# Gate and up projection of two prompt groups as one two by two block product with seven block products

## The chip, the cores and the metric

The kernel runs on one NeuronCore of a Trainium2 chip. The metric is the device time of one execution in microseconds. The engines are TensorE (PE in the profile, with its weight loads as PEld), VectorE (DVE), ScalarE (ACT), GpSimd (POOL) and SyncE (SP), which here only issues DMA transfers. The engines run side by side, each takes its own instructions in a fixed order, and semaphores join them.

## What is computed

One encoder layer is applied to 1536 tokens of width 1024: a prompt of 1024 and a sample of 512 tokens, with the same weights and a modulation vector of their own each. The change lies in the second half of the layer, and what surrounds it is this:

```python
x = x + gt1 * rms_norm(mix, g_post_mix)          # mix: output projection, 1024 x 1024
h = rms_norm(x, g_pre_ffn) * (1.0 + sc2) + sh2
gate, up = jnp.split(jnp.dot(h, w_gu), 2, axis=-1)   # w_gu: 1024 x (2 * 2816)
f = jnp.dot(jax.nn.silu(gate) * up, w_down)          # w_down: 2816 x 1024
return x + gt2 * rms_norm(f, g_post_ffn)
```

## The kernel before

The tokens are three groups of 512 (`TG`): groups 0 and 1 are the prompt, group 2 the sample. Activations lie transposed, channels on the 128 partitions and the 512 tokens of a group along the row, so that one matmul takes a 128 x 128 weight block and 512 columns. All weights and activations are float32. To keep their precision, `split` (lines 137 to 139) writes each operand as two fp32r tiles: ACT casts the high part, and DVE (or POOL, where the caller says so) subtracts it from the source for the low part. `mm3` (line 158) then makes three matmuls for each 128-row chunk of K: high weight with high activation, high with low, low with high. A block over K = 1024 is 8 chunks, 24 matmuls, and fills one PSUM bank; PSUM has 4 banks under the tag mm, 2 under st and 2 under pv.

`weights` (line 141) loads a weight tile through SP into `wraw` (4 buffers of 128 x 512) and splits it into `whl` (4 buffers), so PE runs one block of 1024 behind the splits.

`out_proj(gi)` makes the output projection of a group, 8 blocks (`mt`). `post` (line 794) evacuates each block twice on ACT (lines 806 and 807: scaled into `sc`, squared into `ta`) and adds up the squares on DVE (line 190). Work that belongs to a group but need not hold PE up is a generator on `self.back`, of which `tick(n)` issues n steps after each block. After an output projection such a generator, `behind`, follows: row scale (`rms`: a small matmul, a reciprocal root on DVE L215 and POOL L216, and `spread` over ACT L227, a matmul and ACT L232 into a tile `rs`, 2 buffers), then for each of 8 chunks a multiplication by the row scale (L819), the addition of the residual from DRAM (L820), the store of `x1` (L821), a square on ACT (L823) and the sum of squares on DVE (L838); at its end `rs2[gi]`, the row scale of the second norm, from a second `rms`.

`ffn_in(gi)` (line 890, through `modulate`, line 374) loads the chunks of `x1` into `xc` (3 buffers), scales them (DVE L380, ACT L382) and splits them (ACT, POOL) into 8 tiles of `h` (16 buffers of 128 x 2 x 512). For group 0 it is woven step by step with the `behind` of group 1, during the output projection of group 2; for groups 1 and 2 it runs during the down projection of the group before.

`ffn(gi)` (line 894) has two stages. Gate and up: for each of 22 columns j a gate and an up block over `h2`, then silu (ACT L907, DVE L908) and the product with up (DVE L909), split at once into a tile that stays in SBUF (`HID` names the buffers it borrows). Down: 8 blocks of 22 chunks, 66 matmuls each, into `post`. The last quarter of the adaLN modulation (`ada_rest((5,))`) is fed in between columns 4 to 7.

What is written here is not the order on the engines. The tile framework plans the instructions: on each engine the next is, among those whose inputs and buffers are ready by its own model, the one that stands first in the program; that order is then fixed, and a buffer's next use waits for its last reader. Matmuls of a later block can so come ahead of one whose operand is late.

## Time and profile before

| | us |
|---|---|
| median of 3 runs (1886.78 to 1887.4) | 1886.98 |
| the profiled execution | 1886.02 |
| its span | 1884.2 |

| engine | busy us | share of the span |
|---|---|---|
| PE | 1846.7 | 98% |
| PEld | 1471.2 | 78% |
| DVE | 928.3 | 49% |
| ACT | 690.6 | 37% |
| POOL | 149.0 | 8% |

The span runs from the first to the last instruction of the profiled execution; times in views are microseconds from its start. The group projections and attention fill it to about 610 us, the three output projections to about 751, and then come the three groups' gate and up stages (from about 751, 1130 and 1499) and down stages. A matmul's duration in a view contains its way through the array, and neighbouring ones overlap: their cost to a full PE is the distance from start to start. The same holds for DVE instructions, which overlap a little.

### The profile page before, as it was taken

To read this page: it belongs to the slowest core of one execution; us is meant where nothing else is said; L and a number is where in the kernel's file an instruction comes from. 1 tells how busy PE (TensorE), PEld (TensorE's weight loads), DVE (VectorE), ACT (ScalarE), POOL (GpSimd) and SP (SyncE) were. 2 spreads that over 40 slices of the span, in tenths; PEclk is the share of its full clock that TensorE was granted. 3 is DMA by queue.
4 is the path that set the end of the run, shared out by engine and by line. 5 is a ranking of instruction groups with operands and counts; after the bars stand their busy time and mean duration, and the time that the engine had idled before them with its cause. 6 is when DMAs were issued, how large, how long until landed. Compare 5 with 4: busy or idle time off the path is not lost.

```text
span 1884.2 us, 23515 instructions
## 1 busy us (share of the span) xinstructions
PE 1846.7 (98%) x8866; PEld 1471.2 (78%) x8866; DVE 928.3 (49%) x1447; ACT 690.6 (37%) x1180; POOL 149.0 (8%) x102
## 2 busy tenths in 40 slices
PE   7999999999999999999999999999999999999997
PEld 7777876766777777878888888888888888888886
DVE  4334864473795467834443427444442374444223
ACT  3511642152444456533333423333342333333222
POOL 1400100010122012100000100000020000000001
PEclk9999999999999999999999999999999999999999
DMA  8112322234353367642223435322243342222432
GB/s 340 38 55 76 110 95 93 90 118 134 111 176 114 132 218 217 213 162 92 97 94 108 123 94 181 109 95 95 95 122 97 95 169 97 93 95 95 137 96 75
DMA packets 123682, 228.30 MB, mean 121 GB/s; under 512 B 13744, under 2 KB 19120, under 8 KB 123568
## 3 DMA queue, kind: packets, MB, share of 16 engines
q1 hardware_dynamic: 123424, 226.73, 36.2%
q8 instruction: 69, 1.13, 0.2%
q14 instruction: 45, 0.37, 0.1%
q10 hardware_dynamic: 144, 0.07, 0.0%
HBM read 206.30 MB, written 20.45 MB: 120 GB/s over the span
## 4 chain that ended last, share of the span: by engine, by line
PE 59%; DVE 0%; POOL 0%; DVEq 0%; ACT 0%; issue 0%
PE pmm L156 58%; PE pst L156 1%; DVE sc L861 0%; DVE sc L863 0%; POOL rq L216 0%; DVE whl L139 0%; DVEq L1054 0%; ACT tb L227 0%; DVE rq L215 0%
## 5 line engine op out<-in xcount | busy, mean ns | idle before, releaser
L156 PE MATMUL pmm<-h,whl 128*128 128x512 f32 x5772 | 1384.2, 398 | 11.7 <-ACT h L138 5.2
L156 PEld LDWEIGHTS pmm<-h,whl 128*128 128x128 f32 x5772 | 1079.1, 189 | 288.6 <-issue 22.6
L139 DVE TENSOR_TENSOR whl<-wraw,whl 128x512 fp32r<-128x512 f32 (+1 forms) x548 | 386.0, 707 | 461.3 <-ACT whl L138 458.1
L138 ACT CAST whl<-wraw 128x512 fp32r<-128x512 f32 (+1 forms) x548 | 333.2, 609 | 674.4 <-PE pmm L156 558.5
L139 POOL TENSOR_TENSOR h<-tb,h 128x512 fp32r<-128x512 f32 x40 | 59.6, 1497 | 554.9 <-ACT h L138 546.7
L156 PE MATMUL pmm<-qk,whl 128*128 128x512 f32 x414 | 100.0, 394 | 0.0
L908 DVE SCALAR_TENSOR_TENSOR ta<-ta,pmm 128x512 f32<-128x512 f32 x66 | 45.4, 687 | 110.8 <-ACT ta L907 110.7
L156 PEld LDWEIGHTS pmm<-qk,whl 128*128 128x128 f32 x414 | 77.8, 188 | 18.3
L907 ACT ACTIVATE ta<-pmm 128x512 f32<-128x512 f32 x66 | 39.5, 598 | 141.4 <-PE pmm L156 141.4
L909 DVE SCALAR_TENSOR_TENSOR ta<-ta,pmm 128x512 f32<-128x512 f32 x66 | 45.3, 687 | 79.2 <-PE pmm L156 79.0
L190 DVE TENSOR_TENSOR acc<-acc,ta 128x512 f32<-128x512 f32 x55 | 38.6, 702 | 55.4 <-ACT ta L807 44.3
L156 PE MATMUL pst<-qk 64*128 64x128 f32 (+3 forms) x384 | 61.7, 320 | 0.7 <-DVE st L782 0.7
L156 PEld LDWEIGHTS pst<-qk 64*128 64x128 f32 (+1 forms) x384 | 45.6, 187 | 20.1 <-issue 14.3
L216 POOL TENSOR_TENSOR rq<-rq,half 128x4 f32<-128x4 f32 (+1 forms) x11 | 11.7, 1068 | 526.6 <-DVE rq L215 521.9
L382 ACT ACTIVATE tb<-tb,mod,G 128x512 f32<-128x512 f32 x48 | 38.8, 815 | 39.8 <-DVE tb L380 36.0
L156 PE MATMUL pmm<-v,whl 128*128 128x512 f32 x207 | 51.4, 392 | 0.0
L139 POOL TENSOR_TENSOR h<-xc,h 128x512 fp32r<-128x512 f32 x24 | 33.7, 1414 | 171.3 <-ACT h L138 155.1
L806 ACT ACTIVATE sc<-pmm,G 128x512 f32<-128x512 f32 x47 | 32.2, 686 | 40.8 <-PE pmm L156 40.6
L156 PEld LDWEIGHTS pmm<-v,whl 128*128 128x128 f32 x207 | 38.8, 188 | 8.8
L460 DVE SCALAR_TENSOR_TENSOR sc<-cst,pst 128x512 f32<-128x512 f32 (+2 forms) x56 | 26.9, 512 | 37.8 <-PE pst L156 37.7
L620 POOL PARTITION_ALL_REDUCE st<-st x8 | 21.0, 2637 | 224.1 <-DVE st L556 224.1
L156 PE MATMUL pst<-h,qk 128*128 128x128 f32 x256 | 31.8, 286 | 7.0 <-DMA h<-in_wada 6.8
(163 smaller groups left out, 1299.6 us busy)
## 6 DMA issues: line engine op xcount, KB each, us to landing
wraw<-in_wgu SPq DMA_DIRECT2D x264, 256.0 KB, 2.7
wraw<-in_wdn SPq DMA_DIRECT2D x120, 256.0 KB, 2.6
wraw<-in_win SPq DMA_DIRECT2D x84, 256.0 KB, 2.8
xc<-in_wada SPq DMA_DIRECT2D x48, 256.0 KB, 3.7
wraw<-in_wout SPq DMA_DIRECT2D x48, 256.0 KB, 3.0
xc<-in_x SPq DMA_DIRECT2D x40, 256.0 KB, 3.6
xc<-x SPq DMA_DIRECT2D x40, 256.0 KB, 3.7
h<-in_wada SPq DMA_DIRECT2D x16, 512.0 KB, 9.6
```

Source lines behind the costliest of these rows:

```text
L138: self.nc.scalar.copy(hi, src)
L139: (eng or self.nc.vector).tensor_tensor(out=lo, in0=src, in1=hi.bitcast(F32), op=ALU.subtract)
L156: self.nc.tensor.matmul(out, lhsT, rhs, start=start, stop=stop, skip_group_check=True)
L190: nc.vector.tensor_tensor(out=acc, in0=acc, in1=t, op=ALU.add)
L216: nc.gpsimd.tensor_tensor(out=y, in0=y, in1=self.half8[:, :n], op=ALU.pow)
L382: nc.scalar.activation(t, t, AF.Identity, bias=sh[:, kc, c:c + 1], scale=G[:, kc, c:c + 1])
L460: self.nc.vector.scalar_tensor_tensor(out=out, in0=table, scalar=slope, in1=ps, op0=ALU.mult, op1=ALU.add)
L620: self.nc.gpsimd.partition_all_reduce(x[:, :grp.n], x[:, :grp.n], channels=128, reduce_op=RED.max)
L806: nc.scalar.activation(ys[-1][:, mt % 2], ps, AF.Copy, scale=G[:, mt, c:c + 1])
L907: nc.scalar.activation(t, ps[0], AF.Tanh, scale=0.5)
L908: nc.vector.scalar_tensor_tensor(out=t, in0=t, scalar=1.0, in1=ps[0], op0=ALU.add, op1=ALU.mult)
L909: nc.vector.scalar_tensor_tensor(out=t, in0=t, scalar=0.5, in1=ps[1], op0=ALU.mult, op1=ALU.mult)
```

## The change

Gate and up of column j are a weight block of 2 x 2 (A11, A12: the two K halves of gate; A21, A22: those of up) against an activation block of 2 x 2 (B11, B12: the first K half of groups 0 and 1; B21, B22: the second). Instead of eight products of half blocks seven are made, of sums and differences of the A and of the B (the form named after Strassen and Winograd), and the four results come out of sums of the seven. Groups 0 and 1 go through gate and up together; group 2 goes as before.

- `wino_in` takes the place of the two `ffn_in`: for each of 4 pairs of chunks it makes the tiles of B11, T2, B21, T3, T1 (20 tiles, in the buffers that `OPS` names) and stores T4 and B22 in DRAM (`late`). It stands on `self.back` behind the `behind` of group 1, no longer woven with it, and runs during the third output projection. `wino_late` loads T4 and B22 again and splits them into `h` once the third output projection is through.
- `wino_weights` forms the four sums of the weights on DVE and splits seven operands, in `whl` and `sc` by turns. Raw tiles come in two sets by the parity of j: `wraw` with one of `xc`, and `sd`.
- `wino_products` makes the seven products, 12 matmuls each, into three PSUM banks, some of them added to what a bank holds.
- `ffn_up` reads the banks between the products, makes the silu and the gating step of both groups, and stores the activations in DRAM (`hid`). The split of the activations is no longer there.
- `ffn_down(gi)` loads the 22 activations of a group, splits them into the buffers of `HIDP` and makes the down projection, which is the old one under the name `down`.

```diff
@@ __init__
+        self.hid = self.dr.tile([2, NJ, 128, TG], F32, name="hid")
+        self.late = self.dr.tile([2, 4, 128, TG], F32, name="late")
...
+    OPS = ["h"] * 8 + ["qk"] * 6 + ["v"] * 3 + ["vm"] * 2 + ["sc"]
+    HIDP = ["h"] * 8 + ["qk"] * 6 + ["v"] * 3 + ["vm"] * 2 + ["sc"] + ["st"] * 2
...
+    def wino_in(self, ops):
+
+        nc = self.nc
+        rs = [self.spread(self.rs2[gi], True) for gi in range(2)]
+        for o in ("B11", "T2", "B21", "T3", "T1", "T4", "B22"):
+            ops[o] = []
+        for k in range(4):
+            B = {}
+            for kk in range(2):
+                pair = self.t("st", [128, 2, 512])
+                for gi in range(2):
+                    kc = k + 4 * kk
+                    x = self.load_chunk(self.x1[gi, :, kc])
+                    t = pair[:, gi]
+                    nc.vector.tensor_tensor(out=t, in0=x, in1=rs[gi], op=ALU.mult)
+                    nc.scalar.activation(t, t, AF.Identity, bias=self.mod[:, 3, kc, 0:1], scale=self.G[2][:, kc, 0:1])
+                    B[kk, gi] = t
+                yield
+            B11, B12, B21, B22 = B[0, 0], B[0, 1], B[1, 0], B[1, 1]
+            T1, T2 = self.t2("ta"), self.t2("ta")
+
+            def keep(o, src, eng):
+                i = 4 * ("B11", "T2", "B21", "T3", "T1").index(o) + k
+                h = self.t(self.OPS[i], [128, 2, 512], F32R)
+                self.split(h[:, 0], h[:, 1], src, eng)
+                ops[o].append(h)
+            keep("B11", B11, nc.gpsimd)
+            self.sub(T1, B12, B11)
+            self.sub(T2, B22, T1)
+            keep("T2", T2, nc.vector)
+            yield
+            keep("B21", B21, nc.gpsimd)
+            self.sub(B12, B22, B12)
+            keep("T3", B12, nc.vector)
+            yield
+            keep("T1", T1, nc.gpsimd)
+            self.sub(B21, B21, T2)
+            nc.sync.dma_start(out=self.late[0, k], in_=B21)
+            nc.sync.dma_start(out=self.late[1, k], in_=B22)
+            yield
+
+    def wino_late(self, ops):
+        for i, o in enumerate(("T4", "B22")):
+            for k in range(4):
+                x = self.load_chunk(self.late[i, k])
+                h = self.t("h", [128, 2, 512], F32R)
+                self.split(h[:, 0], h[:, 1], x)
+                ops[o].append(h)
+
+    def wino_weights(self, raw, s3):
...
+            w = self.t("whl" if n % 2 == 0 else "sc", [128, 2, 512], F32R)
...
+        yield op(A11)
+        self.sub(s3, A11, A21)
+        self.nc.vector.tensor_tensor(out=A21, in0=A21, in1=A22, op=ALU.add)
+        self.sub(A11, A21, A11)
+        yield op(A11)
+        yield op(A12)
+        self.sub(A12, A12, A11)
+        yield op(s3)
+        yield op(A21)
+        yield op(A22)
+        yield op(A12)
+
+    def wino_products(self, w, ops, fresh):
+
+        for o, bank, first in (("B11", 0, True), ("T2", 1, True), ("B21", 0, False), ("T3", 1, False),
+                               ("T1", 2, True), ("T4", 1, False), ("B22", 2, False)):
+            if first:
+                fresh[bank] = self.p("pv" if bank == 2 else "mm")
+            wt = next(w)
+            for k in range(4):
+                c = slice(128 * k, 128 * k + 128)
+                h = ops[o][k]
+                ps = fresh[bank]
+                self.mm(ps, wt[:, 0, c], h[:, 0], first and k == 0, False)
+                self.mm(ps, wt[:, 0, c], h[:, 1], False, False)
+                self.mm(ps, wt[:, 1, c], h[:, 0], False, k == 3)
+            yield
+
+    def ffn_up(self, ops):
...
+        def silu(t, g):
+            nc.scalar.activation(t, g, AF.Tanh, scale=0.5)
+            nc.vector.scalar_tensor_tensor(out=t, in0=t, scalar=1.0, in1=g, op0=ALU.add, op1=ALU.mult)
+
+        def gated(t, u, gi, j):
+            nc.vector.scalar_tensor_tensor(out=t, in0=t, scalar=0.5, in1=u, op0=ALU.mult, op1=ALU.mult)
+            nc.sync.dma_start(out=self.hid[gi, j], in_=t)
+        for j in range(NJ):
+            if j >= 4:
+                next(self.ada, None)
+            if j % 2 == 0:
+                raw = [self.t2("wraw") for _ in range(4)]
+                s3 = self.t2("xc")
+            else:
+                a, b = self.t("sd", [128, 3, 512]), self.t("sd", [128, 3, 512])
+                raw, s3 = [a[:, 0], a[:, 1], a[:, 2], b[:, 0]], b[:, 1]
+            for i in range(4):
+                nc.sync.dma_start(out=raw[i], in_=self.a["wgu"][2 * j + i // 2, :, 512 * (i % 2):512 * (i % 2) + 512])
+            ps = {}
+            steps = self.wino_products(self.wino_weights(raw, s3), ops, ps)
+            next(steps)
+            p1 = self.t2("tb")
+            nc.scalar.copy(p1, ps[0])
+            next(steps)
+            e = self.t("st", [128, 2, 512])
+            e6, e67 = e[:, 0], e[:, 1]
+            add(e6, p1, ps[1])
+            next(steps)
+            t0 = self.t2("ta")
+            silu(t0, ps[0])
+            next(steps)
+            add(e67, p1, ps[1])
+            next(steps)
+            add(e67, e67, ps[2])
+            next(steps)
+            add(p1, p1, ps[1])
+            gated(t0, p1, 0, j)
+            next(steps)
+            add(e6, e6, ps[2])
+            t1 = self.t2("acc")
+            silu(t1, e6)
+            gated(t1, e67, 1, j)
+            self.tick(1)
+
+    def ffn_down(self, gi, nxt):
+        hid = []
+        for j in range(NJ):
+            x = self.load_chunk(self.hid[gi, j])
+            h = self.t(self.HIDP[j], [128, 2, 512], F32R)
+            self.split(h[:, 0], h[:, 1], x)
+            hid.append(h)
+        if nxt is not None:
+            self.back.append(self.ffn_in(gi + 1, nxt))
+        self.down(gi, hid)
...
-        self.post(gi, product, self.G[3], self.x1[gi], self.a["y"][gi], False, 2)
+        self.post(gi, product, self.G[3], self.x1[gi], self.a["y"][gi], False, 2 if gi != 1 else 3)
...
-        h2 = [[], [], []]
-        self.back.append(weave(self.back.pop(), self.ffn_in(0, h2[0])))
+        ops, h2 = {}, []
+        self.back.append(self.wino_in(ops))
         self.out_proj(2, hs[2], 4)
         self.tick(-1)
+        self.wino_late(ops)
         self.ada = self.ada_rest((5,))
-        for gi in range(NG):
-            self.ffn(gi, h2[gi], h2[gi + 1] if gi + 1 < NG else None)
+        self.ffn_up(ops)
+        self.ffn_down(0, None)
+        self.ffn_down(1, h2)
+        self.ffn(2, h2)
         self.tick(-1)
```

## Rows read from the trace of the kernel before

**Rows 1.** The page: busy time by engine, and the last chain's shares by line.
```profile
PE 1846.7 (98%) x8866; PEld 1471.2 (78%) x8866; DVE 928.3 (49%) x1447; ACT 690.6 (37%) x1180; POOL 149.0 (8%) x102
...
PE pmm L156 58%; PE pst L156 1%; DVE sc L861 0%; DVE sc L863 0%; POOL rq L216 0%; DVE whl L139 0%; DVEq L1054 0%; ACT tb L227 0%; DVE rq L215 0%
```
**Rows 2.** Windows: busy us (count) of PE, PEld, DVE, ACT, POOL, clock, DMA share, GB/s.
```profile
700.00:751.00 51.00, 46.55 (x201) 36.87 (x202) 38.96 (x52) 32.37 (x61) 15.43 (x11) 0.97 0.69 214
751.00:1006.00 255.00, 254.29 (x1140) 203.89 (x1139) 123.03 (x198) 92.19 (x161) 7.95 (x6) 1.00 0.39 130
775.00:800.00 25.00, 25.00 (x109) 20.28 (x108) 22.53 (x37) 12.60 (x22) 0.00 (x0) 1.00 0.77 273
1006.00:1130.00 124.00, 124.00 (x541) 100.62 (x540) 45.03 (x64) 46.58 (x80) 12.73 (x8) 1.00 0.37 111
```
**Rows 3.** Waits of PE from 751 to 1868 us: total us, times, longest.
```profile
PE pmm L156 <- DVE whl L139: 0.7, 1, 0.7
```
**Rows 4.** Timeline, gate and up of group 0: start us, us, engine, line, operation.
```profile
964.23 0.69 DVE L909 SCALAR_TENSOR_TENSOR ta<-ta,pmm 128x512 f32<-128x512 f32 x1 [1.40 <-PE pmm L156]
...
975.39 0.69 DVE L909 SCALAR_TENSOR_TENSOR ta<-ta,pmm 128x512 f32<-128x512 f32 x1 [1.40 <-PE pmm L156]
```
**Rows 5.** Timeline of PE, down of group 0: first chunks of two neighbouring blocks.
```profile
1040.17 2.22 PE L156 MATMUL pmm<-v,whl 128*128 128x512 f32 x9
...
1055.46 2.22 PE L156 MATMUL pmm<-v,whl 128*128 128x512 f32 x9
```
**Rows 6.** Timeline of DVE: work behind output projections 0 and 2.
```profile
663.58 4.91 DVE L819 TENSOR_TENSOR sc<-sc,rs 128x512 f32<-128x512 f32 x8 [0.64 <-ACT rs L232]
...
773.04 4.91 DVE L819 TENSOR_TENSOR sc<-sc,rs 128x512 f32<-128x512 f32 x8 [0.99 <-ACT rs L232]
...
780.27 0.68 DVE L909 SCALAR_TENSOR_TENSOR ta<-ta,pmm 128x512 f32<-128x512 f32 x1
...
795.26 1.49 DVE L838 TENSOR_TENSOR acc<-acc,tb 128x512 f32<-128x512 f32 x2
```
**Rows 7.** Groups by line and shape, whole span: count, busy us, mean ns, idle before.
```profile
L156 PE MATMUL pmm<-h,whl 128*128 128x512 f32 x5736 | 1379.2, 398 | 11.7 <-ACT h L138 5.2 <-DVE whl L139 4.2 <-DVE h L139 1.4
...
L138 ACT CAST whl<-wraw 128x512 fp32r<-128x512 f32 x524 | 323.5, 619 | 633.7 <-PE pmm L156 517.8 <-issue 101.1 <-DMA wraw<-in_win 5.5
...
L139 POOL TENSOR_TENSOR h<-tb,h 128x512 fp32r<-128x512 f32 x40 | 59.6, 1497 | 554.9 <-ACT h L138 546.7 <-PE pmm L156 7.2 <-POOL h L139 0.7
```
**Rows 8.** DMA issues: count, KB each, median us from issue to landing.
```profile
wraw<-in_wgu SPq DMA_DIRECT2D x264, 256.0 KB, 2.7
...
xc<-mix SPq DMA_DIRECT2D x24, 256.0 KB, 3.1
x<-sc SPq DMA_DIRECT2D x24, 256.0 KB, 3.8
```
**Rows 9.** Timeline of ACT: sixth of eight evacuations of the third output projection.
```profile
739.95 0.69 ACT L806 ACTIVATE sc<-pmm,G 128x512 f32<-128x512 f32 x1 [0.73 <-PE pmm L156]
```
**Rows 10.** Timeline of POOL: reciprocal roots of the row scales.
```profile
655.92 1.45 POOL L216 TENSOR_TENSOR rq<-rq,half 128x4 f32<-128x4 f32 x1 [40.34 <-DVE rq L215]
...
692.94 1.39 POOL L216 TENSOR_TENSOR rq<-rq,half 128x4 f32<-128x4 f32 x1 [3.35 <-PE pmm L156]
...
704.14 1.01 POOL L216 TENSOR_TENSOR rq<-rq,half 128x4 f32<-128x4 f32 x1 [1.29 <-PE pmm L156]
...
763.80 1.98 POOL L216 TENSOR_TENSOR rq<-rq,half 128x4 f32<-128x4 f32 x2 [2.47 <-DVE rq L215]
```
**Rows 11.** Timeline: a POOL split and the DVE split beside it.
```profile
722.03 1.51 POOL L139 TENSOR_TENSOR h<-tb,h 128x512 fp32r<-128x512 f32 x1 [7.24 <-ACT h L138]
722.34 1.75 DVE L139 TENSOR_TENSOR whl<-wraw,whl 128x512 fp32r<-128x512 f32 x1
```
**Rows 12.** Windows behind PE's idle stretch at the start, columns as in rows 2.
```profile
44.00:46.00 2.00, 0.43 (x2) 0.43 (x3) 2.00 (x4) 0.57 (x1) 2.00 (x2) 0.50 0.00 0
...
50.00:52.00 2.00, 2.00 (x6) 1.60 (x5) 0.64 (x1) 1.30 (x2) 1.92 (x3) 0.50 0.00 0
52.00:54.00 2.00, 2.00 (x8) 1.58 (x8) 0.75 (x2) 1.48 (x3) 1.56 (x2) 0.78 0.00 0
```

More of the change, by code (lines that the diff above doesn't have):

```diff
@@ new lines, in wino_late, with op @@
+    def wino_late(self, ops):
[6 more added lines that the diff above has]
+    def wino_weights(self, raw, s3):
+        A11, A12, A21, A22 = raw
+        n = 0
+        def op(src):
+            nonlocal n
+            w = self.t("whl" if n % 2 == 0 else "sc", [128, 2, 512], F32R)
+            n += 1
+            self.split(w[:, 0], w[:, 1], src)
+            return w
+        yield op(A11)
[9 more added lines that the diff above has]
+        yield op(A12)
@@ new lines, in ffn_up @@
+    def ffn_up(self, ops):
+        nc = self.nc
+        add = lambda o, a, b: nc.vector.tensor_tensor(out=o, in0=a, in1=b, op=ALU.add)
+        def silu(t, g):
[40 more added lines that the diff above has]
+            self.tick(1)
@@ L913, in ffn, with down @@
             self.tick(1)
-        if nxt is not None:
-            self.back.append(self.ffn_in(gi + 1, nxt))
+        self.down(gi, hid)
+    def down(self, gi, hid):
         def product(mt, halves=False):
```

4 lines of the change are left out of this document (3 added, 1 removed).

## Prediction

> **What bounds the kernel now.** I read the page first: PE is busy 98% of the span and the chain that ended last consists of L156 matmuls alone wherever it can be followed [rows 1]. Then the windows by stage: over the gate and up stage of group 0 (751 to 1006 us) PE is busy 254.29 of 255 us at full clock while DVE is at 123 and ACT at 92, and in the down stage behind it PE has all of 124 us [rows 2]. Then the waits: from 751 to 1868 us PE waited 0.7 us in total [rows 3]. So time is TensorE instructions times their pitch, and any other engine matters only where it falls behind. The pitch: two gating steps of neighbouring columns stand 964.23 and 975.39, so a column of 48 matmuls of 512 takes 11.16 us, 232.5 ns each [rows 4]; a down block of 66 takes 15.29 us, 231.7 ns each [rows 5].
>
> **What is taken from PE.** Before, one column j of both prompt groups costs 2 x 48 = 96 matmuls. After, it is seven products of four K chunks with three matmuls each, 84. Over 22 columns that is 264 fewer, 264 x 232.5 ns = **-61.4 us**, all on the path because PE has no idle time there. A column then takes 84 x 232.5 = 19.53 us against 22.32.
>
> The Trainium skill (TensorE: Matmul & The Clock Gate, Back-to-back issue gap) gives N / 2.4 + 2.5 ns, 216 ns for 512 columns; by it the cut would be worth 57.0 us, an estimate from that page, and the end 4.4 us later. The rows have the longer pitch, and they decide.
>
> **The steady column on the other engines.** DVE does per column 7 splits, 4 weight sums, 5 output sums and 4 gating steps, 20; before it did 14 for the two groups. DVE instructions that follow one another without a wait step at 4.91 / 8 = 0.61 us [rows 6], so 20 are 12.2 us of 19.53. ACT has 7 casts, a copy and 2 tanh, 10 against 12, about 0.62 us each [rows 7]: 6.2 us. SP issues 4 loads and 2 stores where it issued 8 loads; a store stands in SP's queue ahead of later weight loads and waits for the gating step, but two sets of raw weight buffers give those loads most of a column of slack and a load lands 2.7 us after its issue [rows 8]. New are hand-overs inside a column: the third product writes bank 0 again and must wait for ACT's copy of it, the fourth and sixth wait for DVE's sums of bank 1, the seventh for the sum of bank 2. In each case another product of 2.79 us lies between, and DVE's answer takes one running and one own instruction, 1.2 to 1.4 us. I take **0**, and the range up to 0.3 us a column, 6 us; below nothing it cannot go, since PE is already full. The four adaLN steps of the stage share buffers (tb, xc) with the new tiles: **+1 us** (0 to 4).
>
> **The entry, the main cost.** Before, PE goes from the third output projection to gate and up at 751: the sixth of its eight evacuations waited for PE until 739.95 [rows 9], and two blocks of 24 x 232.5 ns follow. The operands of group 0 were made beside it, and only those were needed. Now the first product needs sums over both groups, so it needs the row statistics of group 1, which come out of the work behind output projection 1. For group 0 that work, not woven with anything, ran from the first reciprocal root at 655.92 to the second, ended 694.33: 38.4 us [rows 10]. For group 1 the first is at 704.14, so the second would end at 742.5 (before, woven with ffn_in, it ended at 765.8); with the spread over ACT, PE and ACT again, about 6 us as from 657.4 (655.92 + 1.45) to 663.58 [rows 6, 10], wino_in starts in earnest at about 748, three microseconds before PE wants its result.
>
> Per chunk pair wino_in has 10 DVE, 9 ACT and 3 POOL instructions, 4 loads and 2 stores; four pairs are 40 DVE = 24.4 us, and 12 POOL splits. A POOL split of 1.5 us [rows 7] holds DVE up: at 722.03 one starts, and the DVE split beside it takes 1.75 us instead of 0.69 [rows 11]. That is up to 1.06 us for each, 12.7 us. The Trainium skill (SBUF — State Buffer, Who interferes with whom) says that this pair of ports is an exclusive lock, which speaks against three POOL splits a pair; by it each would cost DVE its whole 1.5 us, 18 us, an estimate that puts the end 5 us later. The row shows a part of the instruction still overlapping, so I keep 1.06.
>
> What DVE has to do from 748 until the first column is finished, in the order of the program, which is the order its queue prefers among ready work: rest of the projection 2; wino_in 24.4 + 12.7; wino_late 8 splits, 4.9; weights of column 0, 11 instructions, 6.7; the work behind projection 2 (normalise, add, square sums), 24 instructions, 14.6; column 0's own sums, 9, 5.5. That the fourth is taken first is seen before: eight L819 stand in one run from 773.04 and the gating step of a column came only at 780.27 [rows 6]. It cannot start until wino_in gives back a row-scale buffer (rs, 2 of them, both held), about 780, and took 773.0 to 796.8 before, paced by its loads, so I let a third of it fall behind column 0: 9.7 instead of 14.6. Of wino_in, the group 0 half of the first pair needs no group 1 statistics and runs in DVE's gap ahead of 748: -3. Sum 2 + 37.1 + 4.9 + 6.7 + 9.7 + 5.5 - 3 = 62.9 us, so column 0 ends at about 811. Without a stall it would have ended at 751 + 19.5 = 770.5. **+40 us.** In these 60 us PE has 84 matmuls to do, 19.5 us; chunks 0 to 2 of the first, second and fifth products can go ahead, but nothing that shortens DVE's list.
> Bounds: if all of the fourth item falls behind column 0 and POOL costs half, 62.9 - 9.7 - 6.4 = 46.8, a loss of 24; if none of it does and DVE idles in wino_in (a pair's tiles come back only after its stores have landed, 2 to 4 us [rows 8]) 10 us more, a loss of 55.
>
> While PE waits its clock falls: after the idle stretch before 46 us it was granted 0.50 (1.2 of 2.4 GHz) until 52 and 0.78 to 54, beside running matmuls [rows 12]. Half clock inside the stall costs nothing more; of these 7 us I let 4 fall behind it, which cost half: **+2 us** (0 to 4). DVE is not short afterwards: 7.3 us a column are free.
>
> **Up to down.** Activations go to DRAM and come back: 44 stores, 44 loads, 44 ACT and 44 DVE splits, 22 of each group in front of its down product instead of inside the columns. For group 0 the slots come free from the end of the first product of the last column, 16.7 us before PE wants the first. Loads go through xc, 3 buffers; a turn is 3.1 us for a load from DRAM like that of mix [rows 8] + 0.62 [rows 7] + 0.69 [rows 4] + about 0.3 for the hand-overs, 4.7 us, so a tile each 1.6 us. The last of 22 is there -16.7 + 1.3 + 19 x 1.6 = 15 us after the switch (3 wait in xc), wanted after 21 x 0.70 = 14.6. DVE has 9 + 22 + 8 instructions, 24 us, in 32. **+3 us** (0 to 10). For group 1 eight tiles load early into the other h slots, the rest come free during the last down block and are wanted 15 us later: **+1 us** (0 to 4). ffn_in(1) goes away from the down stage, where it was hidden: 0. ffn_in(2) moves behind group 1's activations: DVE is busy 45 of 124 us there [rows 2], 0.
>
> **Sum.** -61.4 + 40 + 2 + 1 + 3 + 1 = -14.4. The profiled execution took 1886.0 us (span 1884.2 and 1.8 around it), 1.0 under the median of 1887.0: 1871.6 there, **1872** as a median to a microsecond.
>
> **Rivals.** *Entry mostly hidden*: the planner lets the work behind projection 2 slip, and POOL collides little. For it: DVE was idle for a quarter of 700 to 751 [rows 2], and PE can take parts of products early. Against: DVE was already 22.5 of 25 us busy at 775 to 800 with far less to do [rows 2]. Loss about 20: 1852.
> *Late hand-overs in each column, slower than before*: two of the four bank hand-overs wait for one more DVE instruction with its ACT cast ahead of it, 0.7 us each: 22 x 1.4 = 31 us, 1903. It decides from 14.4 / 22 = 0.65 us a column on, where the whole gain is gone. For it: DVE goes from 48% (123 of 255) to 62% busy, its queue is strict and mixes the next column's weights with this one's sums. Against: 1.4 us of slack at each hand-over.
> *The cut does not reach the time*: a product is 12 matmuls instead of 24, and if PE drained at each seam (a matmul takes 398 ns [rows 7], pitch 232.5), 154 seams x 0.17 = 26 us go, 1898. Against: 44 seams in a stage before, with no idle time [rows 3].
>
> **How the numbers follow.** Forecast 0.50 (1858 to 1886 by its own bounds); entry hidden 0.22; late hand-overs 0.20; seams 0.03; the remaining 0.05 is a forecast with the switch to down worse than 10 us, near 1888. A measurement tells about 0.2% from no change, 3.8 us. Of the forecast's half, 0.47 lies under 1883. So faster 0.22 + 0.47 = 0.69, same 0.03 + 0.05 + 0.04 (late hand-overs that just eat the gain) = 0.12, slower 0.19. The range goes from 1848, the hidden entry, to 1895: it leaves out about 0.05 below and 0.14 above.
>
> **What would show it.** 8602 matmuls instead of 8866; columns at 19.5 us from the third on; the first gate and up products between 751 and about 811 with PE idle for DVE and ACT; PE waits of under 5 us at each down. Wrong it is if PE waits within later columns, if the second statistics of group 1 come well before or after 742, or if the loss at the entry is under 24 or over 55.

## The result, and the profile after

The changed kernel took **1905.2 us** (1903.67 to 1906.86, 4 runs) where the kernel before took 1887.19 beside it: ratio 1.0092, 95% interval 1.0075 to 1.0108. It is 0.9% slower, an interval clear of no change; the forecast was 1872. The profiled execution took 1904.19 us, its span 1902.4, 18.2 more than the span before.

The page of the changed kernel: engines' busy time over the whole span (share) and instructions.
```profile
PE 1800.8 (95%) x8602; PEld 1424.6 (75%) x8602; DVE 1051.9 (55%) x1655; ACT 692.3 (36%) x1192; POOL 142.2 (7%) x98
```
Beside [rows 1], PE has the forecast 264 matmuls less, but only 45.9 us less work, not 61.4: 15.5 us were matmuls that took longer. And PE was idle for 101.6 us where it had been idle for 37.5, 64.1 more; 64.1 - 45.9 is the 18.2.

Where it idles is in the windows (columns as in [rows 2]), the entry and most of the columns:
```profile
751.00:840.00 89.00, 32.80 (x105) 24.46 (x106) 68.52 (x98) 44.47 (x76) 20.12 (x14) 0.62 0.44 145
840.00:1260.00 420.00, 420.00 (x1830) 335.30 (x1829) 272.70 (x434) 126.77 (x223) 0.00 (x0) 1.00 0.27 94
```
From 840 us on PE is busy all of 420 us at the full clock. From 751 to 840 it is idle for 56.2 of 89 us, and where it works its mean granted clock is 0.62 of 2.4 GHz. DVE, which the prediction took for the bound of that stretch, is not full: 68.5 of 89. So something other than the amount of DVE's work sets the length. The waits of PE from 751 to 850 us (total us, times, longest), the largest five:
```profile
PE pmm L158 <- ACT tb L1011: 20.1, 1, 20.1
PE pmm L158 <- ACT h L140: 16.4, 2, 8.4
PE pmm L158 <- ACT ta L809: 6.9, 1, 6.9
PE ppv L158 <- ACT whl L140: 6.3, 1, 6.3
PE pst L158 <- DVE acc L192: 3.4, 1, 3.4
```
The longest single wait, 20.1 us, is for a copy of one PSUM bank, 0.57 us of ACT's time. Why it came so late is read from three timelines. ACT (start, duration, then line and operation): the evacuation of the seventh block of output projection 2, the last three squares (of its sixth to eighth block), the last square of the work behind it, and that copy:
```profile
750.33 0.67 ACT L808 ACTIVATE sc<-pmm,G 128x512 f32<-128x512 f32 x1
...
767.91 0.58 ACT L809 ACTIVATE ta<-pmm 128x512 f32<-128x512 f32 x1
...
777.93 0.58 ACT L809 ACTIVATE ta<-pmm 128x512 f32<-128x512 f32 x1
...
788.52 0.58 ACT L809 ACTIVATE ta<-pmm 128x512 f32<-128x512 f32 x1
...
816.57 0.63 ACT L825 ACTIVATE tb<-sc 128x512 f32<-128x512 f32 x1 [2.78 <-DVE sc L822]
817.11 0.57 ACT L1011 COPY tb<-pmm 128x512 f32<-128x512 f32 x1
```
DVE, same columns: the last sum of those squares, the start of the work behind projection 2, its last sum:
```profile
791.05 0.68 DVE L192 TENSOR_TENSOR acc<-acc,ta 128x512 f32<-128x512 f32 x1
...
798.28 4.91 DVE L821 TENSOR_TENSOR sc<-sc,rs 128x512 f32<-128x512 f32 x8 [4.37 <-ACT rs L234]
...
817.23 0.69 DVE L840 TENSOR_TENSOR acc<-acc,tb 128x512 f32<-128x512 f32 x1 [0.76 <-ACT tb L825]
```
SP: the loads of the T4 and B22 chunks back from DRAM:
```profile
812.20 0.38 SPq L239 DMA_DIRECT2D xc<-late  x1
...
816.87 7.65 SPq L239 DMA_DIRECT2D xc<-late  x6
```
Read together they are **a chain, not a list of work**. Its first link is the order of the squares. wino_in and the squares of output projection 2 draw on the same three `ta` tiles, and the program issues the two in turns. The last squares come 10 us apart, one for each chunk pair, each within 0.5 us of that pair's T2: 767.91, 777.93, 788.52. That they stand there for want of a `ta` tile is argued from the program, and no run tests it by itself. In the trace no `ta` tile was in use from 771.8 to 774.7 us, the block that the square of 777.93 reads had been evacuated at 750.33, and ACT was idle for 2.6 us before 773.19. So what held that square on the chip was its place in ACT's fixed order, behind the pair's scalings. The links behind it are buffers. The sum of squares is therefore complete only at 791.7, the work behind projection 2 starts at 798.28 (6 us of root and spread later) and, instead of running beside wino_in, runs after it. Its squares hold both `tb` tiles, and column 0's copy wants a `tb`: 817.11. Its residual loads hold `xc`, and the T4 and B22 loads want `xc`: 812 to 824.5. Column 0's s3 wants an `xc` too and comes behind those, so PE waits another 6.3 us for split weights, until 829.76. Experiments 1 and 2 test the `tb` and the `xc` link.

The copies of columns 2 and 3 have the pitch of the forecast, 19.50 us. With the adaLN matmuls among them those of columns 3 to 8 stand 15.0 to 25.6 us apart, and from column 8 on (990.93) each follows 19.4 to 19.5 us behind the last:
```profile
865.73 0.59 ACT L1011 COPY tb<-pmm 128x512 f32<-128x512 f32 x1 [3.98 <-PE pmm L158]
...
885.23 0.59 ACT L1011 COPY tb<-pmm 128x512 f32<-128x512 f32 x1 [4.90 <-PE pmm L158]
```

### The profile page after: what moved, and what is told of

Read it like the earlier page. It is cut to its first block, busy times and chain, and to the rows that moved or that the text cites. A ratio compares the mean times of both kernels' runs of the same rounds, so it can differ in the third digit from the quotient of the medians.

```text
span 1902.4 us, 23113 instructions
## 1 busy us (share of the span) xinstructions
PE 1800.8 (95%) x8602; PEld 1424.6 (75%) x8602; DVE 1051.9 (55%) x1655; ACT 692.3 (36%) x1192; POOL 142.2 (7%) x98
## 4 chain that ended last, share of the span: by engine, by line
PE 50%; DMA 4%; DVE 3%; ACT 1%; issue 1%; SPq 0%; POOL 0%; DVEq 0%; ACTq 0%; POOLq 0%
PE pmm L158 43%; PE ppv L158 6%; DMA xc<-hid 1%; DMA xc<-x 1%; PE pst L158 1%; DMA xc<-late 1%; DVE whl L141 0%; DVE st L911 0%; DMA xc<-in_x 0%; DVE sc L821 0%; DMA wraw<-in_wdn 0%; DVE h L141 0%; ACT h L140 0%; DVE sc L863 0%; ACT st L912 0%
## 5 line engine op out<-in xcount | busy, mean ns | idle before, releaser
L158 PE MATMUL pmm<-h,whl 128*128 128x512 f32 (+1 forms) x3924 | 959.5, 399 | 40.5 <-ACT h L140 22.2
L158 PEld LDWEIGHTS pmm<-h,whl 128*128 128x128 f32 x3924 | 728.0, 189 | 241.6 <-ACT h L140 24.7
L141 DVE TENSOR_TENSOR whl<-wraw,whl 128x512 fp32r<-128x512 f32 (+1 forms) x416 | 289.3, 699 | 328.6 <-ACT whl L140 328.3
L140 ACT CAST whl<-wraw 128x512 fp32r<-128x512 f32 (+1 forms) x416 | 251.2, 607 | 507.6 <-PE pmm L158 379.9
L158 PE MATMUL pmm<-qk,whl 128*128 128x512 f32 x678 | 168.5, 399 | 22.5 <-ACT tb L1011 20.1
L158 PEld LDWEIGHTS pmm<-qk,whl 128*128 128x128 f32 x678 | 128.4, 190 | 55.1 <-ACT tb L1011 20.4
L158 PE MATMUL pmm<-h,sc 128*128 128x512 f32 x528 | 131.1, 397 | 0.0
L158 PEld LDWEIGHTS pmm<-h,sc 128*128 128x128 f32 x528 | 99.1, 189 | 24.4 <-DVE ta L991 0.8
L158 PE MATMUL ppv<-h,whl 128*128 128x512 f32 x264 | 65.1, 395 | 0.0
L158 PEld LDWEIGHTS ppv<-h,whl 128*128 128x128 f32 x264 | 49.6, 188 | 12.0
```

Source lines behind the costliest of these rows:

```text
L140: self.nc.scalar.copy(hi, src)
L141: (eng or self.nc.vector).tensor_tensor(out=lo, in0=src, in1=hi.bitcast(F32), op=ALU.subtract)
L158: self.nc.tensor.matmul(out, lhsT, rhs, start=start, stop=stop, skip_group_check=True)
```

## The experiments

Two theories stood at the start. **Buffers**: the entry is a serial chain over ta, tb and xc as above. **DVE list** (the prediction's): it is as long as DVE's work. Times are single runs unless a range is given; "before" is the kernel before on the same chip, 1887.28 us for the first four kernels, 1890.16 for the next six. The kernel before, run seven times on a third chip, took 1885.09 to 1891.66 us, so a difference of a few us between single runs decides nothing without the trace.

**1. The copy takes ta instead of tb.**
```diff
-            p1 = self.t2("tb")
+            p1 = self.t2("ta")
```


> One line: the copy of the first bank (p1) takes a buffer of ta instead of tb. The changed kernel takes 1905; in its trace the third product of column 0 waits 20.1 us for that copy, which ends 817.7. Theory buffers (the copy waits for a tb that the squares behind output projection 2 hold): the copy comes at about 790 and the third product at 792; the column still needs the late tiles (xc, to 827) and its other weights (829 on), so its end stays near 840 and the time falls by 0 to 5 us. Theory DVE list (the column is held by DVE's work alone): the copy, an ACT instruction, comes when it comes today, after 815, and the time stays within 2 us.


1910.3 us. Copies of columns 0 and 1, and PE's largest waits from 751 to 880:
```profile
794.58 0.58 ACT L1011 COPY ta<-pmm 128x512 f32<-128x512 f32 x1
...
847.24 0.59 ACT L1011 COPY ta<-pmm 128x512 f32<-128x512 f32 x1 [2.12 <-PE pmm L158]
```
```profile
PE pst L158 <- DVE acc L840: 19.8, 1, 19.8
...
PE ppv L158 <- ACT whl L140: 9.2, 1, 9.2
```
The copy came 22.5 us earlier, so `tb` did hold it. But nothing was gained: PE now waited 19.8 us at the statistic of the work behind projection 2, which stands in its queue in front of the rest of column 0, and 9.2 for weights. Column 1 came 6 us later than in the changed kernel. The expected gain, 0 to 5 us, was wrong; one wait was taken out of a chain and the next link showed.

**2. Column 0's weights in sd**, which nothing else wants then, by exchanging the two weight sets.
```diff
-            if j % 2 == 0:
+            if j % 2 == 1:
```


> The two sets of raw weight buffers change parity: even columns use sd, odd ones wraw and one xc. Theory buffers: column 0's sums no longer wait for a buffer of xc behind the residual and late loads, its weights are split before 800, only T4 and B22 (818 to 828) still hold its sixth and seventh product: its end moves from 840 to about 833, the time falls by 5 to 8 us. Theory DVE list: the same instructions are merely done earlier, in DVE's gaps: also a fall, of up to 7 us (11 instructions of 0.61). This run does not tell the two apart; it prices the weights of column 0.


1892.66 us, 12.5 less, more than expected. The copies:
```profile
825.18 0.59 ACT L1011 COPY tb<-pmm 128x512 f32<-128x512 f32 x1
...
827.09 0.58 ACT L1011 COPY tb<-pmm 128x512 f32<-128x512 f32 x1
```
The `tb` wait stayed (19.9 us), but with the weights of two columns at hand PE did the first products of both in the stall, and column 1's copy came 14 us earlier. So column 0's wait for an `xc` cost up to 12.5. By what was expected, the same work moved into DVE's gaps could gain up to 7 as well; only what goes beyond that speaks for the buffer.

**3. The work behind projection 2 put off** until the columns run.
```diff
+        last = self.back.pop()
         self.tick(-1)
+        self.back.append(last)
...
-            self.tick(1)
+            self.tick(2)
```


> The work behind output projection 2 is no longer issued ahead of the late tiles and column 0, but two steps after each column. The same instructions in another place. Theory buffers: p1, the late tiles and column 0's weights follow wino_in directly; third product at about 793, late tiles split by about 806, column 0 ended by about 815 instead of 840, and less of it at half clock: the time falls by 25 to 32 us, to 1873 to 1880. Theory DVE list: only the 14.6 us of DVE work that is taken out of the list can be gained: 1890 or more.


1886.92 us, 18.3 less: over what the DVE list allowed (14.6, not by more than single runs differ), under what buffers promised (25 to 32). The trace decides more clearly than the time. PE's timeline at the third product, and the copies of columns 1 to 4:
```profile
792.66 4.50 PE L158 MATMUL pmm<-qk,whl 128*128 128x512 f32 x12 [1.13 <-ACT tb L1011]
```
```profile
818.17 0.59 ACT L1011 COPY tb<-pmm 128x512 f32<-128x512 f32 x1 [1.70 <-PE pmm L158]
...
841.55 0.59 ACT L1011 COPY tb<-pmm 128x512 f32<-128x512 f32 x1 [0.66 <-DVE acc L840]
...
864.12 0.59 ACT L1011 COPY tb<-pmm 128x512 f32<-128x512 f32 x1 [1.39 <-DVE acc L840]
...
895.15 0.59 ACT L1011 COPY tb<-pmm 128x512 f32<-128x512 f32 x1
```
The 20.1 us wait is 1.1 us; the third product comes 25 us earlier (792.66 beside 817.73), with the same DVE work in the kernel. Some 7 us were given back: with the residual work among them columns 1 to 3 take 22.6 to 31 us, not 19.5.

**4. No POOL in wino_in**: its three POOL splits a pair go to DVE.
```diff
-            keep("B11", B11, nc.gpsimd)
+            keep("B11", B11, nc.vector)
```
(and so for B21 and T1)


> The twelve POOL splits of wino_in go to DVE. Theory lock (a POOL split costs DVE up to 1.06 us, an own DVE split 0.61): a pair of chunks takes 10.6 us now with three POOL splits; it falls by 3 x 0.45 = 1.3 us, wino_in ends 5 us earlier and the time falls by 5 us. Rival (the pair is a chain of waits from the stores back to the next pair's tiles, not DVE's list): the period stays within 0.5 us of 10.6 and the time within 2 us.


1901.24 us, 4 less. DVE's first operations of the third and fourth pair, in the changed kernel and then here:
```profile
772.38 1.90 DVE L911 TENSOR_TENSOR st<-xc,rs 128x512 f32<-128x512 f32 x3
...
782.97 1.89 DVE L911 TENSOR_TENSOR st<-xc,rs 128x512 f32<-128x512 f32 x3
```
```profile
774.82 1.90 DVE L911 TENSOR_TENSOR st<-xc,rs 128x512 f32<-128x512 f32 x3
...
784.54 1.90 DVE L911 TENSOR_TENSOR st<-xc,rs 128x512 f32<-128x512 f32 x3
```
A pair takes 9.7 instead of 10.6 us: 0.9 less, between the 1.3 of the first theory and the 0.5 of the rival. How POOL holds DVE is seen in the third pair of the changed kernel, a POOL split and the DVE difference beside it:
```profile
778.26 1.72 POOL L141 TENSOR_TENSOR qk<-st,qk 128x512 fp32r<-128x512 f32 x1
...
778.78 1.75 DVE L895 TENSOR_TENSOR st<-st 128x512 f32<-128x512 f32 x1
```
The DVE operation, 0.69 us elsewhere in the pair, ends 0.55 us behind the end of the POOL split, and so does the one in [rows 11]. So it stood still for nearly all of the time that the two overlapped. The lock that the Trainium skill describes (SBUF — State Buffer, Who interferes with whom) says the same of the port pair that DVE and POOL share; these rows agree with it but for 0.1 us. A price for each split does not follow from the length of a pair: in the third pair DVE's operations took 1.4 us longer, but DVE was also idle for 2.2 us of the pair, and for 1.0 us in the run without POOL. PE's wait for `tb` stayed 19.6 us, as a chain would have it.

**5. No column takes sd.** The output of out projection 1 was late before the entry began: its root of the row scale fell at 708.09 us where it had been 704.14 [rows 10]. The root of projection 0 was late already, 660.68 beside 655.92 [rows 10], so the 4 us arise ahead of it; from 500 to 550 us PE was idle for 3.6 us where it had been for 1.7. The planner had moved column 1's weight loads and sums into the attention stage.
```diff
-            if j % 2 == 0:
+            if True:
```


> All 22 columns take their raw weights from wraw (and s3 from xc), none from sd; nothing else differs from the changed kernel. Theory early lift: the planner moves the weight loads and the first sums of column 1 (4 transfers at 478 us, DVE sums at 485 us) into the attention stage because sd is free there, and that cost the 4 us that out projection 1 ends late; without sd in the columns the statistic of out projection 1 should fall at 701.3 us (as before) instead of 705.3. Theory elsewhere: the 4 us have another cause, and it stays at 705.3. The columns themselves lose half of their buffers; time by the first theory 1901 if they still run at 19.50 us, more if not.


1900.09 us, near the 1901 of the first theory, but the root on POOL is not where that theory puts it:
```profile
707.87 1.01 POOL L218 TENSOR_TENSOR rq<-rq,half 128x4 f32<-128x4 f32 x1 [1.27 <-PE pmm L158]
```
It did not come back to 704.14, so the early lift is not the cause of these 4 us. In the other kernels the same code ahead of this point gave roots from 704.62 (experiment 8) to 714.67 (experiment 12). What spreads them **stays open**.

**6. Pass behind the projection, no detour over DRAM.** wino_in is issued after output projection 2, T4 and B22 are split directly, the residual work is put off as in 3, and the first five columns keep their weights out of sc.
```diff
-        self.back.append(self.wino_in(ops))
         self.out_proj(2, hs[2], 4)
+        last = self.back.pop()
         self.tick(-1)
-        self.wino_late(ops)
+        self.back.append(self.wino_in(ops))
+        self.tick(-1)
+        self.back.append(last)
...
-            nc.sync.dma_start(out=self.late[0, k], in_=B21)
-            nc.sync.dma_start(out=self.late[1, k], in_=B22)
+            for o, x in (("T4", B21), ("B22", B22)):
+                h = self.t("h", [128, 2, 512], F32R)
+                self.split(h[:, 0], h[:, 1], x)
+                ops[o].append(h)
```


> The pass that makes the sums of both groups is issued behind out projection 2, not beside it (so its T1, T2 take ta behind the squares), T4 and B22 are split straight into h without the DRAM round trip, the residual work of out projection 2 waits until the columns run (two steps a column), and the first five columns take their split weights from whl alone. Theory buffers: the chain ta, tb, xc is gone; the pass still starts at 752 with 10.6 us a pair step, so column 0's copy comes near 790 and column 1's some 20 us later; 1870 to 1880. Theory DVE list: the vector engine's work up to the end of column 0 shrinks only by the residual work and the 8 reloaded splits (about 14.6 us in all for the former), 1885 to 1891.


1887.16 us, 18 less than the changed kernel: the DVE list's figure (1885 to 1891), not that of buffers (1870 to 1880). PE in the entry, the first matmul of the second to fourth pair, and below it the copies of columns 0 and 1:
```profile
777.97 0.79 PE L158 MATMUL pmm<-h,whl 128*128 128x512 f32 x1 [9.61 <-ACT h L140]
...
788.98 0.79 PE L158 MATMUL pmm<-h,whl 128*128 128x512 f32 x1 [8.43 <-ACT h L140]
...
800.04 0.79 PE L158 MATMUL pmm<-h,whl 128*128 128x512 f32 x1 [8.44 <-ACT h L140]
```
```profile
804.50 0.59 ACT L1014 COPY tb<-pmm 128x512 f32<-128x512 f32 x1 [0.50 <-PE pmm L158]
...
824.24 0.59 ACT L1014 COPY tb<-pmm 128x512 f32<-128x512 f32 x1 [1.80 <-PE pmm L158]
```
The chain is gone: PE waits for little but the pass itself, a pair each 11 us, and column 1 follows column 0 at 19.7 us, near the steady pitch. In the pass DVE is now nearly full, 17.2 of 20 us:
```profile
770.00:790.00 20.00, 2.81 (x4) 1.07 (x4) 17.23 (x24) 12.74 (x21) 7.36 (x5) 0.50 0.28 86
```
So each theory has its part: the order and the buffers made the chain behind the pass, and for the pass itself DVE's work is close to the bound. It also began late here: the second root fell at 754.01 us, and the root of projection 1 was
```profile
712.30 1.01 POOL L218 TENSOR_TENSOR rq<-rq,half 128x4 f32<-128x4 f32 x1 [1.25 <-DVE rq L217]
```

**7 to 11. What fills the stall.** If the order of the work is the cause, an order that does not make group 0 wait for group 1 should win. Five kernels go there in steps. In the first, B11 and B21, which need group 0 alone, are issued beside output projection 2, and columns 0 and 1 run their A11 B11 and A12 B21 products ahead of the rest:
```diff
+        self.back.append(self.wino_first(ops, raws))
         self.out_proj(2, hs[2], 4)
+        rs = self.spread(self.rs2[1], True)
+        cols = [self.column(j, ops, True) for j in range(2)]
+        for _ in range(2):
+            for c in cols:
+                next(c)
+        self.wino_second(ops, raws, rs)
```


> The same without the wait of group 0 for group 1: B11 and B21 of group 0 are made and split beside out projection 2 (raw copies kept in sd and sc), the first two columns run A11 B11 and A12 B21 ahead of the rest (4 blocks of 12 matmuls, 11 us of PE), and only B12, B22 and the sums of group 1 are left behind the second root; POOL splits 2 of 5 of these. Theory order of work: the stall is as long as the chain from the second root to the last operand, now some 30 us by DVE (44 operations of 0.69 us), less the 11 us of products that fill it; 1855 to 1866. Theory half clock: once PE has idled, it is the slow clock, not the missing operands, that costs, and the gain over v_direct is under 5 us.


1881.87 us. One wait stood out, over 745 to 900 us:
```profile
PE pmm L158 <- ACT whl L140: 23.9, 3, 18.0
```
The weights of the next product were issued behind the whole second pass, and DVE made them last. The pass over group 0, too, ran only from 752.77 us on, behind the projection. The time, 1855 to 1866 by the theory, was missed; the 5 us below experiment 6 are no more than single runs differ. The same kernel with the last adaLN part run in the stall:
```diff
-        self.ada = self.ada_rest((5,))
+        for _ in self.ada_rest((5,)):
+            pass
```


> w_early, with the last adaLN part run right behind out projection 2 instead of in the columns from the fifth on: 11 us of PE (the same instructions) moved into the stall. Theory order of work: 6 to 11 us below w_early. Rival: its 16 weight transfers take xc and tb from the group 1 chunks, and it ends within 3 us of w_early or behind it.


1884.77 us: the rival held. Its root of projection 1 was the earliest of all changed kernels, but the loads of its 16 weight tiles, most of them into `xc`, were issued until 774.1 us, those of group 1's chunks into `xc` only from 776.39 on, and the wait for the weights grew to 27.4 us:
```profile
704.62 1.01 POOL L218 TENSOR_TENSOR rq<-rq,half 128x4 f32<-128x4 f32 x1 [1.15 <-DVE rq L217]
```
```profile
815.17 1.22 PE L158 MATMUL pmm<-h,whl 128*128 128x512 f32 x2 [27.39 <-ACT whl L140]
```
Without the adaLN part, and with the T2 weights of both columns made ahead of the second pass:
```diff
-        for _ in range(2):
+        for _ in range(3):
             for c in cols:
                 next(c)
```
(the third step of a column only makes those weights; their s3 moves from `xc` to `acc`)


> w_early, but the weights of the T2 product of both early columns are summed and split ahead of the second pass (in w_early they stood behind it in the vector engine's list and the tensor engine waited 18 us for them), with their s3 in acc instead of xc. Theory order of work: PE then takes T2 operand by operand while the pass runs, and the 18 us wait shrinks to what the pass itself still needs: 1864 to 1872. Rival, DVE list: the 8 operations are only moved, the last operand comes 5 us later, and the gain is at most what the two T2 products are long (5.6 us): 1876 to 1880.


1883.54 us, neither theory's figure: no gain at all. The 18 us wait was gone, but two others of the same length in sum had come, from 745 to 900 us:
```profile
PE pmm L169 <- ACT h L151: 8.6, 3, 5.2
PE pmm L169 <- ACT whl L151: 8.6, 2, 7.8
```
Over the whole span PE was idle for 67.1 us instead of 71.7, but its 8602 matmuls were busy for 1814.6 us instead of 1808.4: the shorter wait was paid back by longer matmuls, at a granted clock of 0.66 from 800 to 820 us instead of 0.76. Whether that clock held up anything, this run does not show.

Then group 0's pass was woven with the residual work of projection 1, and POOL left the second pass:
```diff
-        self.back.append(self.wino_first(ops, raws))
+        self.alongside(self.wino_first(ops, raws))
...
-            self.keep(ops, k, "T1", T1, self.nc.gpsimd)
+            self.keep(ops, k, "T1", T1)
```
(and so for B22, in an order that frees `xc` sooner)


> y_noada, with the pass over group 0 issued alternately with the residual work of out projection 1 instead of behind it (in w_early it ran only from 752.8 us on, so 15 of the vector engine's 19 us from 751 on went to it), and the five splits a step of the second pass all on the vector engine, in an order that frees xc sooner. Theory order of work: group 0's operands are made before 752, the second pass ends some 10 us earlier, and the time falls by 6 to 12 us below y_noada. Rival: the pass over group 0 delays the residual work, the second root (751.6 us in w_early) comes as much later as the pass is shorter, and nothing is gained (within 3 us of y_noada).


1877.59 us, 6 less, at the near edge of the theory's 6 to 12, though the rival's effect was there too: the second root came at 760.07, not 751.62. PE still waited 7.8 us for column 2's weights:
```profile
837.70 1.22 PE L169 MATMUL pmm<-h,whl 128*128 128x512 f32 x2 [7.81 <-ACT whl L151]
```
Last, the residual work of projection 2 let in only behind column 2 (the first eight columns also take their split weights from `whl` alone):
```diff
-        self.back.append(last)
+        self.last = last
...
+            if j == 2:
+                self.back.append(self.last)
             self.tick(2)
```


> y_weave, with the residual work of out projection 2 let in from the fourth column on instead of from the first (and the first eight columns' split weights from whl alone, since its y tiles hold sc). In y_weave PE waited 7.8 us at 837.7 us for column 2's weights, whose sums stood behind 8 residual multiplications of 0.6 us each. Theory order of work: that wait goes, and no new one comes: 1868 to 1873. Rival: the residual work has the same 17 operations wherever it stands and only moves the wait to column 4 or so: within 2 us of y_weave's 1877.6.


**1864.1 us** (1862.97 to 1864.53, 4 runs) beside 1886.87: ratio 0.9872, 95% interval 0.9855 to 0.9888, faster than both kernels. Its entry as a window, and PE's largest waits from 820 us to the end:
```profile
751.00:820.00 69.00, 50.76 (x181) 36.60 (x180) 55.06 (x91) 30.36 (x54) 2.72 (x2) 0.80 0.15 50
```
```profile
PE pst L169 <- ACT tb L240: 3.0, 1, 3.0
PE pmm L169 <- DVE whl L152: 1.6, 1, 1.6
```
The wait for column 2's weights did not return anywhere. The kernel computes the same seven products a column with the same 8602 matmuls. So 41 us of the changed kernel's time lay not in PE's work but in when the work around it was issued, which buffers it shared, and in two smaller things that went with it, the way of T4 and B22 over DRAM and the POOL splits.

**12 and 13. Is the slow clock a cost of its own?** After an idle stretch PE works at the lower level, 1.2 GHz, and its busy time was 15.5 us too long. First, matmuls that nobody reads were put into the changed kernel's entry:
```diff
                 self.split(h[:, 0], h[:, 1], src, eng)
                 ops[o].append(h)
+                self.warm(h, 8)
```


> The changed kernel with matmuls added whose results nobody reads: 8 behind each of the 20 splits of the pass over both groups (same form as the products, 37 us in all at full clock) and 2 behind each of the squares of the residual work of out projection 2, so that PE works through the entry. Theory half clock: the 15 us that the matmuls between 751 and 850 us lost at the 0.5 clock were on the path; the granted clock stays near 1.0 and the time falls to 1890 to 1898. Theory buffers: those matmuls waited for operands anyway, at whatever clock; the time stays at 1901 to 1907, or rises by the added work that the planner puts ahead of products.


1922.1 us. One of its windows, to be held against a clock of 0.52 in the changed kernel:
```profile
770.00:790.00 20.00, 20.00 (x84) 16.02 (x83) 15.87 (x21) 12.61 (x20) 9.40 (x6) 0.95 0.48 158
```
The clock was up and the time went up too. It is no clean test. The added matmuls stood in PE's queue in front of the last block of output projection 2, evacuated at 780.36 instead of 767.34, and of column 0. And the second root fell at 756.43, 9.8 us later than in the changed kernel, ahead of the first added matmul (761.82). So it was done again in the kernel of experiment 6, inside waits that it shows:
```diff
             keep("B11", B11, nc.gpsimd)
+            self.warm(ops["B11"][-1], 16)
...
             keep("T2", T2, nc.vector)
+            self.warm(ops["T2"][-1], 8)
```


> v_direct, in which PE waits four times for the pass, 8.4 to 9.6 us each, and then runs at the 0.5 and 0.7 clock until about 820; added are 24 matmuls of the products' form behind two splits of each pair step, results unread, 5.6 us a step at full clock, so that they lie inside those waits and not ahead of ready products. Theory half clock: the products from 800 to 820 us (15.7 us busy at a mean clock of 0.69) run at full clock and everything behind comes 4 to 6 us earlier relative to the last split of the pass: 1881 to 1884, beside 1887 for v_direct. Theory buffers: those products are paced by the weight splits of DVE anyway, and nothing comes earlier, clock or not: 1886 to 1890.


1884.18 us, before 1884.43 on that chip (ratio 0.9999; experiment 6 had 0.9984 against 1890.16). Against the kernel before there is no gain on experiment 6; the time alone, 3 us less, doesn't decide. The window behind the stall, in experiment 6 and here, then the copies of columns 0 and 1 here:
```profile
800.00:810.00 10.00, 5.71 (x12) 3.72 (x13) 9.57 (x12) 8.45 (x17) 6.43 (x3) 0.50 0.19 55
```
```profile
800.00:810.00 10.00, 10.00 (x40) 8.07 (x38) 9.57 (x13) 5.33 (x10) 4.62 (x3) 0.79 0.24 68
```
```profile
807.46 0.58 ACT L1021 COPY tb<-pmm 128x512 f32<-128x512 f32 x1
...
826.14 0.58 ACT L1021 COPY tb<-pmm 128x512 f32<-128x512 f32 x1
```
The clock was 0.79 instead of 0.50, and 0.84 instead of 0.50 from 770 to 800, yet the copies came 3.0 and 1.9 us later, though the pass's last POOL split started 1.95 us earlier. In the stall the higher clock brought nothing forward: there the next operand set the pace. Behind it the test is not clean either: the last 16 added matmuls kept PE until 804.8 us. **A small cost stays open**, with a bound from the changed kernel's own rows: behind the last long wait PE worked 2.3 us at 0.50 and then, from 820 to 850, 23.7 us at a mean of 0.80; at the full clock 1.1 + 4.7 us less. And the statistic's matmuls on the way to 798.28 took 1.84 and 2.08 us (at 791.87 and 795.55), where the same ones of projection 0 took 0.95 and 1.05 at full clock (at 659.45 and 666.62): 1.9 us. So by this estimate at most 8 of the 15.5 us can have delayed anything. The kernel of experiment 11 points the same way: its matmuls were busy for longer (1804.7 us beside 1800.8), and it is 41 us faster.

## Why the prediction was wrong, point by point

The entry failed, by its mechanism; the rest of the sum held. (The sum, redone, gives 1887.0 - 14.4 = 1872.6 as a median, where 1872 was written.)

- **The cut, -61.4 us**: right. 8602 matmuls, columns at 19.50 us, 232.1 ns for each of 84. By the isolated gap of 216 ns in the Trainium skill (TensorE: Matmul & The Clock Gate, Back-to-back issue gap) a column would have been 18.1 us, an estimate from that page. The trace does not agree: from column 8 on, where nothing else is mixed in, no column took less than 19.4.
- **Steady columns, 0**: right. From 840 to 1260 us PE has no idle time; the hand-overs of banks, the slower-side rival with 1.4 us a column, cost nothing. The seams, too, cost nothing.
- **The switches to down, +4**: right. PE is idle for 0.7 us at 1260 to 1310, 1.1 at 1395 to 1440 and 2.1 at 1440 to 1516, 3.9 together.
- **The second root of group 1 at 742.5**: right up to the shift. It came at 746.68, and projection 1's statistic was 4 us late already, as was projection 0's. That shift of **+4** was no term of the sum; experiment 5 rules out one cause, and none is shown.
- **The entry, +40 and +2**: the step that failed. Column 2's copy was due at 811 + 19.5 + 3.1 = 833.6 us and came at 865.73, 32.1 late; take off the shift of 4, and the entry cost **about 70 instead of 42**. Those 32.1 are the miss but for 0.5 us (1904.2 against 1871.6).
  The list of DVE's work was about right: 62.9 us forecast, 68.5 measured from 751 to 840, some of it for column 1. The inference from it was not: "What DVE has to do ... until the first column is finished" was set equal to the time that it takes. DVE was idle for 20.5 us of the stretch, since the work came to it in a chain. Two sentences carry the error. That the work behind projection 2 "cannot start until wino_in gives back a row-scale buffer", about 780: it started at 798.28, because its statistic needed squares that came one for each chunk pair, the last at 788.52, which the prediction did not look at. And that a third of it would "fall behind column 0": all of it fell ahead of column 0, because the copy of column 0 needs a `tb` that its squares hold. The prediction counted rs and the stores of wino_in as the buffers that bind; it did not count tb and xc, with 2 and 3 tiles, for the three pieces of code that now stand in one stretch, nor the squares that were issued in turns with wino_in. Experiment 1 shows the `tb` link; experiment 2 shows that column 0's weights were on the path, by 12.5 us, of which DVE's gaps could explain 7. Why the squares stood where they did is argued only.
- **POOL beside DVE, 12.7 in the list**: the row was misread. It was said to show "a part of the instruction still overlapping". But the DVE split of [rows 11] began 0.31 us into the POOL split, so only 1.20 us of the two overlapped, and it took 1.06 longer. That is a wait for POOL's end. The sum counted it for every split; in the third pair, where the sum had 3.2 us, DVE's operations took 1.4 us longer.
- **Slow clock**: forecast 2 us, contained in the 42. Of the 15.5 us of extra busy time at most 8 can have delayed anything (experiments 12 and 13), so this term may be short by up to 6; the rest is inside the waits, where the prediction said that "half clock inside the stall costs nothing more".
- **Rivals**: that the entry is mostly hidden did not hold for this code, though its loss can be made small: in the last kernel PE is idle for 18.2 us from 751 to 820. The slower side came true by a mechanism that was not among the rivals: a chain of order and buffers at the entry, not late hand-overs in each column.

## What to carry to other kernels

Where a change puts pieces of code side by side that stood apart, list for each rotating buffer who takes it, in the order of the program, and how many there are, and look for the longest chain through those lists; the sum of an engine's work is only a lower bound. A wait taken out of such a chain can bring nothing by itself (in experiment 1 the copy came 22.5 us earlier and the kernel was 5 us slower), so follow the chain to its end before counting a gain. In-order queues carry a late statistic to everything behind it: put off what nobody needs yet, and make early what needs only half of the inputs.

## What the runs showed of the hardware that was not expected

- Matmuls at the lower clock level cost less than their extra time here: by the estimate above at most 8 of 15.5 us. With PE at 0.84 instead of 0.50 in the stall, column 0's copy still came no earlier (807.46 beside 804.50 us), though the added matmuls that raised the clock took time of their own.
- A DVE operation that ran into a POOL split ended 0.55 us behind the split's end, 1.75 us after its start instead of 0.69 (778.78 us in the changed kernel, 722.34 in [rows 11]).
- The same code ahead of the change's place gave arrival times 10 us apart over the kernels (704.62 to 714.67 for one root), a spread of which the shift of 4 us is a part; its cause is open.
